# A two-layer hybrid trunk on one core: convolution and Fourier inputs as seven-product block multiplications, two conditioning groups on TensorE

## The chip, the cores and the metric

The kernel runs on one core of a Trainium2 chip. The metric is the device time of one execution in microseconds (us), median of three runs. The engines are named as the profile names them: PE is TensorE's matrix multiplication and PEld its weight load, DVE is VectorE, ACT ScalarE, POOL GpSimd, and SP SyncE, which here only issues DMAs.

## The reference

Two layers work on 640 tokens: 512 latent ones in four blocks of 128, and one block of 128 context tokens. The model width is 1024. Per layer:

```
h = LN0(x) * (1 + scale) + shift          # shift, scale, gate = silu(cond) @ w_mod + b_mod
q, k, v, z_a, cb, cc, cx, z_b, fx, z_c, g = split(h @ w_in)
                                          # widths 512,128,128,512, 4 x 512, 512,512, 3 x 1024
y_a = attention(q, k, v) * silu(z_a)      # 8 heads of 64, 2 KV heads, window +-128 and the context
y_b = cb * dwconv3(cc * cx) * silu(z_b)
y_c = Re(FFT2(fx by groups of 128)) * silu(z_c)
merged = sum over b of sigmoid(g_b) * (y_b @ w_branch_b)
x = LN(alpha * x + gate * (merged @ w_o)) * ln_g + ln_b
```

The outputs are the tokens after two layers and each layer's keys and values of the context block. All of it is float32.

## The kernel before

**Products.** Activations lie with channels on the partitions and tokens along the free axis. A float32 product is made of three products of a faster format: each operand is split into a high part (a copy on ACT) and a remainder (a subtraction on DVE, `split`, L147 for weights), and hi·hi, hi·lo and lo·hi are summed in PSUM. The input projection has 58 chunks of 128 columns, and eight k-steps of 128 rows. A plain chunk (`inproj`, `product`, L505 to L507) takes, per k-step, three matmuls of 256 and three of 384 tokens, 48 in all; its weights come in two 128x512 tiles, each of which is split.

**Pairs.** The 24 gate chunks go two at a time through a 2x2 block product with seven multiplications in place of eight (Strassen's scheme). The blocks are the two chunks, the two halves of the input channels, and the two halves of each token block (so 320 tokens). A seventh (L957) is 12 matmuls of 320 columns; three of seven read sums of input blocks, kept in tiles `T` (made by `sums` and `last_sum` on DVE and ACT), and the weights of three are sums of weight blocks (`Sum` on DVE; one sum, s1, by a DMA of POOL's queue that accumulates, L137). Results come in three banks, x, y and z, which ACT copies and DVE adds into two result rows.

**Stages of a layer.** First Q, K and V. Then attention in ten units (token block 0 to 4, KV head 0 or 1; a name ends in layer, block, head, and counter): `scores` on PE (L645), the mask with its maximum on DVE (L648), exponentials on ACT (L670, after a table load) with their sums, the normalisation by the reciprocal on POOL (L676, four instructions a unit); then `values`: four transposes of 128 columns on PE into pt (L694), a copy and subtraction into pT, and the products into po (L699 and L700). Between the units stand the 20 chunks of the A gating path and of the convolution (`fills`). Chunks 26 to 33 are the Fourier branch, each FX chunk followed by its transforms (`channels`, `positions`). Then the gates by pairs, in whose midst the branch projections (pb) are placed, then the output projection and the residual.

**Conditioning.** The shift, scale and gate vectors of both layers come from w_mod, in groups of 512 columns. Layer 0's first ones are done on PE at the start (modp L459, 256 columns, eight matmuls each; then modq). The others are accumulated on DVE: per k-step two instructions of 128x512 (L239, or L236 for the first), then a transpose, a reduction and one matmul. Groups (0,4), (0,5) and (1,0) do so beside layer 0's attention (`mod_steps`, rows `P<-sz`); the remaining ones beside the gates (`mod_piece`, rows `moda<-rawm`).

**Order.** The program is written as a list of jobs; `run` issues weight loads on SP's queue and weight splits as far ahead as six raw and five split tiles allow. The framework's scheduler then fixes each engine's order, so each engine runs its own list in order and waits on semaphores. SBUF is divided into large tiles with letters (A to F), each reused when its last reader is done; row tiles have five buffers. PSUM has two double banks (chunks) and four single ones (`aux`).

## Time and profile before

| | us |
|---|---|
| median of 3 runs (1242.32 to 1243.58) | 1242.64 |
| the profiled execution | 1243.65 |
| its span, first to last instruction | 1241.9 |
| PE busy | 1211.6 |
| DVE busy | 918.7 |
| ACT busy | 568.3 |
| POOL busy | 182.1 |

The span starts with the first instruction. Busy times of different engines lie beside each other. In a timeline, a row's second number is how long one instruction takes from its start to its end; where instructions follow each other without a gap, the distance between two starts is what one costs, and is shorter, since the next begins before the last has drained. A row ends in the idle time before it and what ended it, where there was any. PE's granted clock is given as a share of full speed: its mean over the span is 0.996.

### The profile page before, as it was taken

The numbers are of one execution on the slowest core, as the hardware profiler recorded it, in microseconds if no ns is written. First come the engines' busy times: TensorE is split into PE (matmuls) and PEld (weight loads), VectorE is DVE, ScalarE is ACT, GpSimd is POOL, SyncE is SP. The second block draws the span as 40 slices with busy tenths as digits, with TensorE's granted clock in tenths as the row PEclk, the third lists the DMA queues.
The fourth block names the chain that finished last, engine by engine and source line by source line (L and its number), as shares of the span: only waits on it lengthen the run. The fifth ranks groups of instructions, "written<-read, shape, count | busy, mean of one in ns | idle before, by whom it ended". The sixth has DMA issues, their size and how long they took to land.

```text
span 1241.9 us, 20937 instructions
## 1 busy us (share of the span) xinstructions
PE 1211.6 (98%) x8016; PEld 1166.8 (94%) x8016; DVE 918.7 (74%) x1683; ACT 568.3 (46%) x1100; POOL 182.1 (15%) x180
## 2 busy tenths in 40 slices
PE   5999999999999999999999999999999999999997
PEld 4899999999999999999889999999999999999986
DVE  5795697879799876677888665666869966666766
ACT  4345636456344344463245646545444344445300
POOL 2003424041000000000230324232000000000001
PEclk8999999999999999999999999999999999999999
DMA  9632131313255452453412211112223533433351
GB/s 353 235 113 69 52 119 60 102 60 120 62 160 153 128 151 71 102 174 135 158 72 82 73 56 60 51 55 93 92 57 125 160 111 92 131 88 106 105 187 51
DMA packets 64085, 137.38 MB, mean 111 GB/s; under 512 B 7600, under 2 KB 8176, under 8 KB 63728
## 3 DMA queue, kind: packets, MB, share of 16 engines
q1 hardware_dynamic: 59232, 125.35, 30.5%
q0 software_dynamic: 4176, 10.39, 4.1%
q8 instruction: 63, 1.03, 0.4%
q10 hardware_dynamic: 576, 0.30, 0.1%
q14 instruction: 38, 0.31, 0.1%
HBM read 130.48 MB, written 5.52 MB: 110 GB/s over the span
## 4 chain that ended last, share of the span: by engine, by line
PE 88%; DVE 6%; DMA 2%; issue 2%; ACT 1%; POOL 1%; DVEq 0%; SPq 0%; POOLq 0%
PE y L957 13%; PE p L505 12%; PE p L507 12%; PE p L506 12%; PE z L957 6%; PE pb L505 4%; PE pb L507 4%; PE pb L506 4%; PE x L957 3%; PE pt L694 2%; PE s L645 2%; PE p L422 2%; PE o L1118 2%; PE o L1117 2%; PE o L1119 2%
## 5 line engine op out<-in xcount | busy, mean ns | idle before, releaser
L505 PE MATMUL p<-act,hlw 128*128 128x256 f32 (+1 forms) x1024 | 321.0, 314 | 0.9 <-ACT qr L69 0.9
L507 PE MATMUL p<-act,hlw 128*128 128x256 f32 (+1 forms) x1024 | 318.9, 311 | 0.0
L506 PE MATMUL p<-act,hlw 128*128 128x256 f32 (+1 forms) x1024 | 317.4, 310 | 0.0
L505 PEld LDWEIGHTS p<-act,hlw 128*128 128x128 f32 x1024 | 193.3, 189 | 2.8 <-ACT qr L69 1.2
L506 PEld LDWEIGHTS p<-act,hlw 128*128 128x128 f32 x1024 | 192.8, 188 | 1.5
L507 PEld LDWEIGHTS p<-act,hlw 128*128 128x128 f32 x1024 | 192.8, 188 | 1.3
L676 POOL TENSOR_SCALAR P<-P,rc 128x384 f32<-128x384 f32 (+2 forms) x80 | 115.5, 1459 | 233.2 <-ACT hlw L69 101.4
L69 ACT ACTIVATE hlw<-raww 128x512 fp32r<-128x512 f32 x136 | 85.2, 629 | 109.0 <-PE p L507 97.0
L147 DVE TENSOR_TENSOR hlw<-raww,hlw 128x512 fp32r<-128x512 f32 x134 | 92.4, 693 | 25.0 <-ACT hlw L69 23.9
L1117 PE MATMUL o<-wo,act 128*128 128x512 f32 (+1 forms) x168 | 63.8, 381 | 0.0
L1118 PE MATMUL o<-wo,act 128*128 128x512 f32 (+1 forms) x168 | 63.5, 379 | 0.0
L1119 PE MATMUL o<-wo,act 128*128 128x512 f32 (+1 forms) x168 | 63.1, 379 | 0.0
L72 DVE TENSOR_TENSOR pT<-pt,pT 128x512 fp32r<-128x512 f32 x60 | 40.1, 685 | 20.9 <-ACT pT L69 20.8
L69 ACT ACTIVATE gs<-y 128x320 f32<-128x320 f32 x48 | 20.8, 433 | 67.3 <-PE y L957 66.3
L239 DVE SCALAR_TENSOR_TENSOR moda<-rawm,scond,moda 128x512 f32<-128x512 f32 x70 | 51.0, 742 | 0.0
L69 ACT ACTIVATE pT<-pt 128x512 fp32r<-128x512 f32 x60 | 34.9, 592 | 31.5 <-PE pt L694 25.0
L648 DVE CUSTOM_DVE_ANT_0 P<-s,mask 128x384 f32<-128x384 f32 (+1 forms) x64 | 38.5, 617 | 10.3 <-PE s L645 10.2
L670 ACT ACTIVATE P<-P,nm 128x384 f32<-128x384 f32 (+1 forms) x64 | 42.1, 658 | 1.2 <-DVE es L72 0.7
L75 DVE TENSOR_TENSOR gs<-pb,gs 128x640 f32<-128x640 f32 x16 | 13.2, 825 | 38.6 <-PE pb L507 38.6
L505 PE MATMUL pb<-ya,hlb 128*128 128x256 f32 (+1 forms) x128 | 40.1, 313 | 0.1
L505 PE MATMUL pb<-yc,hlb 128*128 128x256 f32 (+1 forms) x128 | 39.9, 311 | 0.0
L505 PE MATMUL pb<-yb,hlb 128*128 128x256 f32 (+1 forms) x128 | 39.8, 311 | 0.0
(722 smaller groups left out, 2888.5 us busy)
## 6 DMA issues: line engine op xcount, KB each, us to landing
raww<-in_w_in SPq DMA_DIRECT2D x136, 256.0 KB, 2.9
rawm<-in_w_mod SPq DMA_DIRECT2D x36, 512.0 KB, 4.3
rawg<-in_w_in SPq DMA_DIRECT2D x72, 256.0 KB, 3.4
rawb<-in_w_branch SPq DMA_DIRECT2D x48, 256.0 KB, 3.1
rawo<-in_w_o SPq DMA_DIRECT2D x32, 256.0 KB, 3.0
sz<-in_w_mod SPq DMA_DIRECT2D x24, 256.0 KB, 3.0
dft<-in_dft POOLq DMA_DIRECT2D x2, 1542.0 KB, 7.6
x<-in_x SPq DMA_DIRECT2D x5, 512.0 KB, 8.3
```

What stands on the lines that cost most here:

```text
L69: nc.scalar.activation(out, in_, AF.Copy)
L147: eng.tensor_tensor(out=self.hl[:, 1], in0=raw, in1=fr(self.hl[:, 0]), op=ALU.subtract)
L239: nc.vector.scalar_tensor_tensor(out=acc[:, c], in0=w, scalar=scond[:, k, c:c + 1], in1=acc[:, c], op0=ALU.mult, op1=ALU.add)
L505: nc.tensor.matmul(ps[:, a:b], lhsT=ld.w(0, k), rhs=mh, start=k == 0, stop=False)
L506: nc.tensor.matmul(ps[:, a:b], lhsT=ld.w(0, k), rhs=ml, start=False, stop=False)
L507: nc.tensor.matmul(ps[:, a:b], lhsT=ld.w(1, k), rhs=mh, start=False, stop=k == nk - 1)
L670: nc.scalar.activation(P[:, g, :W], srcs[g], AF.Exp, scale=0.125, bias=nm_[:, g:g + 1], accum_out=sm[:, g:g + 1])
L676: nc.gpsimd.tensor_scalar(out=P[:, g, :W], in0=P[:, g, :W], scalar1=rc[:, g:g + 1], scalar2=None, op0=ALU.mult)
L957: nc.tensor.matmul(out, lhsT=ld.w(z, k), rhs=moving(k, y), start=first and k == i == 0, stop=k == 3 and i == 2, skip_group_check=True)
L1117: nc.tensor.matmul(ps, lhsT=act[:, t, 0, k], rhs=w[:, 0], start=k == 0, stop=False)
L1118: nc.tensor.matmul(ps, lhsT=act[:, t, 0, k], rhs=w[:, 1], start=False, stop=False)
L1119: nc.tensor.matmul(ps, lhsT=act[:, t, 1, k], rhs=w[:, 0], start=False, stop=k == NK - 1)
```

## The change

Twelve more pairs per layer use the seven products: for the convolution, CC with CX and ZB with CB of each 128 channels (named c and d, with layer and number), and for the Fourier branch FX and ZC two by two (f). The code of a pair becomes the class `Pair`, with y and z in one double bank; the gates are `Gates(Pair)`. The four ZA chunks stay plain. The sums `T` are made at the start of attention rather than in the Fourier stage, and `fills` places six of a pair's sevenths after each unit. Conditioning groups (0,4) and (0,5) go to PE, 512 columns wide (`mod_group`); group (1,0) goes to the gates' pieces. y_a and y_b are kept unsplit and split beside the gates (`split_y`). The large tiles get other letters, and the loads of w_o other places. In the changed file lines are some six higher: L694 becomes L700, L699 becomes L705, and the line of a seventh, L957, becomes L827.

```diff
+    def mod_group(l, n, tag):
+        w = {}
+        def fetch():
+            w["raw"] = big.tile([128, 4096 if tag == "F" else 5120], F32, name=f"rawm{l}{n}", tag=tag)
+            for kp in range(4):
+                nc.sync.dma_start(out=w["raw"][:, kp * 1024:(kp + 1) * 1024], in_=I["w_mod"][l * 6 + n - 4, kp])
+        def rows():
+            pr = aux(f"modp{l}{n}")
+            for k in range(NK):
+                c = 32 * (k % 4)
+                nc.tensor.matmul(pr[c:c + 32], lhsT=scond32[:, k], rhs=w["raw"][:, k * 512:(k + 1) * 512],
+                                 start=k < 4, stop=k >= 4, tile_position=(0, c))
+            w["rows"] = row(f"modr{l}{n}")[:, 0:512]
+            copy(w["rows"], pr)
+        def columns():
+            ps = aux(f"modq{l}{n}")
+            for i in range(4):
+                nc.tensor.matmul(ps[:, 2 * i:2 * i + 2], lhsT=w["rows"][:, i * 128:(i + 1) * 128], rhs=pick,
+                                 start=True, stop=True)
+            add(modT[:, l, n * 4:(n + 1) * 4, :], ps[:, 0:8].rearrange("p (j s) -> p j s", s=2),
+                bmod[:, l, n * 4:(n + 1) * 4].unsqueeze(2).broadcast_to([128, 4, 2]))
+            mod_scale(l, n)
+        return fetch, rows, columns
...
-            S["ya"] = big.tile([128, 4, 2, TOK], F32R, name=f"ya{l}", tag="C")
-            P = big.tile([128, 5120], F32, name=f"P{l}", tag="E")
+        def begin_scores():
...
+        groups = [mod_group(0, 4, "T"), mod_group(0, 5, "F")] if l == 0 else []
...
-                    mul(ytv, ytv, S["sz"][:, :, tok])
-                    split(S["ya"][:, :, 0, tok], S["ya"][:, :, 1, tok], ytv)
+                    mul(S["sz"][:, :, tok], ytv, S["sz"][:, :, tok])
...
+        class Pair:
+            def __init__(self, nm, c0, c1, begin, done):
+                self.nm, self.begin, self.done, self.G, self.ps = nm, begin, done, [], {}
+                src = [[I["w_in"][l, c][:, h * 512:(h + 1) * 512] for h in range(2)] for c in (c0, c1)]
+                a11, a12 = (Raw(src[0][h], f"g{nm}1{h}") for h in range(2))
+                s1 = Raw(src[1][0], f"g{nm}s", src[1][1])
+                a22 = Raw(src[1][1], f"g{nm}22")
+                def hl(raw, frees, i):
+                    return Split(raw, f"g{nm}p{i}", frees)
+                def old(half, kh):
+                    return lambda k, z: act[:, :, z, 4 * kh + k, 64 * half:64 * half + 64]
+                def new(i):
+                    return lambda k, z: S["T"][i][:, z, k]
+                self.steps = [
+                    (Load([s1, a11, a12, a22], [hl(a11, [], 1)]), "y", old(0, 0), self.keep(0, 0)),
+                    (Load([], [hl(a12, [], 2)]), "x", old(0, 1), self.plus(0, 0)),
+                    (Load([], [hl(s1, [], 5), Sum(add, s1, s1, a11)]), "z", new(0), lambda out: None),
+                    (Load([], [hl(s1, [], 6), Sum(sub, a11, s1, a22), Sum(add, a12, a12, s1, [s1])]), "y", new(1),
+                     self.keep(0, 1)),
+                    (Load([], [hl(a11, [a11], 7)]), "y", new(2), self.third),
+                    (Load([], [hl(a22, [a22], 4)]), "y", lambda k, z: act[:, :, z, k, 64:128], self.last_y),
+                    (Load([], [hl(a12, [a12], 3)]), "z", old(1, 1), self.last_z)]
+            def place(self, bank):
+                if bank == "x":
+                    return aux(f"x{self.nm}")
+                if bank == "y":
+                    self.two = mmt(f"yz{self.nm}")
+                    return self.two[:, 0:512]
+                return self.two[:, 512:1024]
+            def emit(self, n=7):
+                for _ in range(n):
+                    ld, bank, moving, then = self.steps.pop(0)
+                    job(self.product(bank, moving, then), ld)
+            def product(self, bank, moving, then):
+                def body(ld):
+                    first = bank not in self.ps
+                    if first:
+                        self.ps[bank] = self.place(bank)
+                    out = self.ps[bank][:, :320]
+                    for k in range(4):
+                        for i, (z, y) in enumerate(((0, 0), (0, 1), (1, 0))):
+                            nc.tensor.matmul(out, lhsT=ld.w(z, k), rhs=moving(k, y), start=first and k == i == 0,
+                                             stop=k == 3 and i == 2, skip_group_check=True)
+                    then(out.rearrange("p (t i) -> p t i", i=64))
+                return body
+            def keep(self, i, half):
+                def then(out):
+                    if not self.G:
+                        self.G = self.begin()
+                    copy(quarter(self.G[i], half), out)
+                return then
+            def plus(self, i, half):
+                def then(out):
+                    add(quarter(self.G[i], half), out, quarter(self.G[i], half))
+                return then
+            def third(self, out):
+                self.keep(1, 1)(out)
+                self.plus(1, 1)(self.ps["z"][:, :320].rearrange("p (t i) -> p t i", i=64))
+            def last_y(self, out):
+                copy(quarter(self.G[1], 0), out)
+            def last_z(self, out):
+                self.plus(0, 1)(out)
+                self.done(*self.G)
...
+            return [Pair(f"c{l}{j}", C_CC + j, C_CX + j, two_rows("gc"), use_u),
+                    Pair(f"d{l}{j}", C_ZB + j, C_CB + j, two_rows("gd"), use_b)]
+        fill = [p for j in range(4) for p in conv(j) for _ in range(7)]
...
-        side = mod_steps(((0, 4), (0, 5), (1, 0)) if l == 0 else (), lambda: S["moda"], lambda: S["modr"])
...
+                    fill.pop(0).emit(1)
+        if l == 0:
+            job(groups[0][1])
         job(scores(0))
-        fills(2)
+        gating(0)
+        if l == 0:
+            job(groups[0][2])
+            job(groups[1][1])
+        gating(1)
+        if l == 0:
+            job(groups[1][2])
+        job(begin_sums)
+        job(sums(0))
         job(scores(1))
-        fills(1)
+        gating(2)
+        job(sums(1))
         for u in range(10):
             job(values(u))
-            beside(1)
+            if u == 0:
+                gating(3)
+                job(last_sum)
             if u + 2 < 10:
                 job(scores(u + 2))
-                fills(1)
-                beside(1)
-                fills(1)
-                beside(1)
-        beside(99)
+            fills(6 if u else 2)
...
+        def fourier_pair(c, i, use):
+            def begin():
+                return [S["G"][:, i + j] for j in range(2)]
+            g = i % 4
+            return Pair(f"f{l}{i}", c + g, c + g + 1, begin, lambda a, b: use((g, a), (g + 1, b)))
...
-        inproj(l, C_FX, use_fx(0))
-        job(begin_sums)
-        job(sums(0))
-        inproj(l, C_FX + 1, use_fx(1))
-        for g in range(4):
-            job(channels(g))
-            inproj(l, C_ZC + g, use_zc(g))
-            if g == 3:
-                job(last_sum)
-            job(positions(g))
-            if g == 0:
-                job(sums(1))
-            if g < 2:
-                inproj(l, C_FX + g + 2, use_fx(g + 2))
...
+        def split_y(y, tag):
+            def body():
+                w = big.tile([128, 4, 2, TOK], F32R, name=f"s{y}{l}", tag=tag)
+                src = S["sz" if y == "ya" else y]
+                S["s" + y] = w
+                for k in range(4):
+                    split(w[:, k, 0], w[:, k, 1], src[:, k])
...
+        p = fourier_pair(C_FX, 0, use_fx)
+        p.emit()
+        p = fourier_pair(C_ZC, 4, use_zc)
+        p.emit(4)
+        job(channels(0))
+        p.emit(2)
+        job(channels(1))
+        p.emit(1)
+        p = fourier_pair(C_FX, 2, use_fx)
+        p.emit(2)
+        job(positions(0))
+        p.emit(3)
+        job(positions(1))
+        p.emit(2)
+        p = fourier_pair(C_ZC, 6, use_zc)
+        p.emit(3)
+        job(channels(2))
+        p.emit(2)
+        job(channels(3))
+        p.emit(2)
+        job(positions(2))
+        job(positions(3))
+        pieces = [(1, n, kp) for n in (range(4) if l == 0 else (4, 5)) for kp in range(4)]
...
+                if (b, m) == (1, 0):
+                    job(split_y("yb", "C"))
                 piece()
-                if b == 2 and 1 <= m < 3:
-                    load_wo(0, "D", m - 1)
+                if b == 2:
+                    piece()
+                if (b, m) == (0, 1):
+                    job(split_y("ya", "A"))
+                if (b, m) in ((0, 2), (0, 3)):
+                    load_wo(1, "D", m - 2)
```

PE, in attention of layer 0. Before, around the first values of block 2: pt are transposes, po the products that read their copies pT, p0_16 a plain chunk of the convolution.

```order
L699 MATMUL po020_2010<-pT0201_2016,KV0_553 128x512
L694 MATMUL pt0202_2021<-ident_90,P0_560 128x128 x4
L694 MATMUL pt0203_2031<-ident_90,P0_560 128x128 x4
L507 MATMUL p0_16_2159<-act_109,hlw0_16_1_1996 128x384
L505 MATMUL p0_16_2159<-act_109,hlw0_16_1_1996 128x256
L506 MATMUL p0_16_2159<-act_109,hlw0_16_1_1996 128x256
L507 MATMUL p0_16_2159<-act_109,hlw0_16_1_1996 128x256
L505 MATMUL p0_16_2159<-act_109,hlw0_16_1_1996 128x384
L506 MATMUL p0_16_2159<-act_109,hlw0_16_1_1996 128x384
L507 MATMUL p0_16_2159<-act_109,hlw0_16_1_1996 128x384
L505 MATMUL p0_16_2159<-act_109,hlw0_16_1_1996 128x256
L700 MATMUL po020_2010<-pT0201_2016,KV0_553 128x512
```

Between the transposes of pt0202 and the first product that reads pT0202 stand 23 rows, ten of them shown here. After, at the first values of block 1 (yzd00 and yzc01 are sevenths of convolution pairs):

```order
L700 MATMUL pt0100_1601<-ident_90,P0_909 128x128 x4
L705 MATMUL po010_1600<-pT0100_1606,KV0_553 128x512
L827 MATMUL yzd00_1577<-tb0_1100,hlgd00p5_1526 128x320 x12
L827 MATMUL yzd00_1577<-tb0_1100,hlgd00p6_1543 128x320 x11
L700 MATMUL pt0101_1611<-ident_90,P0_909 128x128 x4
L700 MATMUL pt0102_1621<-ident_90,P0_909 128x128 x4
L827 MATMUL yzd00_1577<-tb0_1100,hlgd00p6_1543 128x320
L706 MATMUL po010_1600<-pT0100_1606,KV0_553 128x512
L700 MATMUL pt0103_1631<-ident_90,P0_909 128x128 x4
L705 MATMUL po010_1600<-pT0101_1616,KV0_553 128x512
L706 MATMUL po010_1600<-pT0101_1616,KV0_553 128x512
L651 MATMUL s0200_1644<-KV0_553,Q0_552 128x512 x2
```

The first value product stands directly behind the transposes whose copy it reads, and sevenths behind it.

DVE, in layer 0 between the maxima of the first unit (mx000, ahead of these rows) and those of the second (mx001). The sums of input blocks read `act`; ta, tb and tc are row tiles, tb0 and tf0 the tiles T. All of this stood in the Fourier stage before:

```order
L78 TENSOR_TENSOR ta01_1210<-act_109 128x5x2x64
L78 TENSOR_TENSOR tb01_1211<-act_109 128x5x2x64
L72 TENSOR_TENSOR tb00_1103<-tb00_1103,ta00_1102 128x640
L72 TENSOR_TENSOR tb01_1211<-tb01_1211,ta01_1210 128x640
L72 TENSOR_TENSOR ta00_1102<-tc00_1104,ta00_1102 128x640
L147 TENSOR_TENSOR hlw0_9_1_1086<-raww0_9_1_831,hlw0_9_1_1086 128x512
L72 TENSOR_TENSOR ta01_1210<-tc01_1212,ta01_1210 128x640
L72 TENSOR_TENSOR tb0_1100<-tb00_1103,tb0_1100 128x640
L743 SCALAR_TENSOR_TENSOR tc00_1104<-tc00_1104,tb00_1103 128x640
L72 TENSOR_TENSOR tb0_1100<-tb01_1211,tb0_1100 128x640
L72 TENSOR_TENSOR tf0_1101<-ta00_1102,tf0_1101 128x640
L743 SCALAR_TENSOR_TENSOR tc01_1212<-tc01_1212,tb01_1211 128x640
```

They stand in one piece, with one weight split (hlw0_9_1) among them.

POOL, in layer 0's attention. Before, the normalisations (TENSOR_SCALAR) follow each other with only the convolution's small memsets between:

```order
L676 TENSOR_SCALAR P0_560<-P0_560,rc020_1642 128x512 x4
L730 MEMSET u02_2208 128x2
L731 MEMSET u02_2208 128x1
L676 TENSOR_SCALAR P0_560<-P0_560,rc021_1871 128x512 x4
L676 TENSOR_SCALAR P0_560<-P0_560,rc030_2085 128x384 x4
L730 MEMSET u03_2635 128x2
L731 MEMSET u03_2635 128x1
L676 TENSOR_SCALAR P0_560<-P0_560,rc031_2314 128x384 x4
```

After, the accumulating DMAs of the pairs' weight sums (rawgc02s is that of pair c of layer 0, number 2) stand between them:

```order
L682 TENSOR_SCALAR P0_909<-P0_909,rc020_1672 128x512 x4
L137 DMA rawgc02s_1888<-in_w_in 128x512
L682 TENSOR_SCALAR P0_909<-P0_909,rc021_1863 128x512 x4
L862 MEMSET u01_2071 128x2
L863 MEMSET u01_2071 128x1
L137 DMA rawgd02s_2104<-in_w_in 128x512
L682 TENSOR_SCALAR P0_909<-P0_909,rc030_2052 128x384 x4
L137 DMA rawgc03s_2317<-in_w_in 128x512
L682 TENSOR_SCALAR P0_909<-P0_909,rc031_2248 128x384 x4
```

Each unit's normalisation now has one DMA ahead of it or behind it on POOL's queue.

## Rows read from the trace of the kernel before

**Rows 1.** The page, parts 1 and 2: busy shares; slices in tenths.

```profile
PE 1211.6 (98%) x8016; PEld 1166.8 (94%) x8016; DVE 918.7 (74%) x1683; ACT 568.3 (46%) x1100; POOL 182.1 (15%) x180
...
PE   5999999999999999999999999999999999999997
...
PEclk8999999999999999999999999999999999999999
```

**Rows 2.** PE's waits: line waited for, us in total, times, longest.

```profile
PE tr L342 <- DVE xn L328: 9.8, 2, 9.0
PE tr L342 <- ACT xn L326: 4.3, 2, 2.2
PE y L957 <- ACT gs L69: 2.6, 5, 0.5
```

**Rows 3.** Windows: length, busy us of PE, PEld, DVE, ACT, POOL; clock, DMA.

```profile
83.00:345.60 262.60, 262.47 (x1771) 255.99 (x1771) 206.25 (x419) 139.94 (x282) 65.69 (x59) 1.00 0.27 84
684.20:945.50 261.30, 261.17 (x1760) 254.83 (x1759) 174.30 (x360) 136.85 (x278) 62.12 (x57) 1.00 0.22 69
346.00:425.00 79.00, 76.46 (x516) 75.32 (x514) 76.35 (x126) 32.62 (x62) 3.46 (x4) 1.00 0.52 154
165.00:185.00 20.00, 20.00 (x137) 19.47 (x137) 19.90 (x43) 9.15 (x19) 4.89 (x2) 1.00 0.45 146
```

**Rows 4.** PE's timeline in a plain chunk: start, us.

```profile
67.15 0.34 PE L505 MATMUL p<-act,hlw 128*128 128x384 f32 x1
...
68.04 0.34 PE L505 MATMUL p<-act,hlw 128*128 128x384 f32 x1
```

**Rows 5.** PE's timeline in a gate pair.

```profile
375.38 1.92 PE L957 MATMUL x<-act,hlg012p 128*128 128x320 f32 x12
377.14 0.46 PE L957 MATMUL z<-tb,hlg012p 128*128 128x320 f32 x2
```

**Rows 6.** The chain that ended last, in two stretches: start, us, work.

```profile
22.30 1.01 PE modp L459 x8
...
153.41 0.87 PE pt L694 x8
```

**Rows 7.** DVE's timeline, in three stretches.

```profile
131.65 0.69 DVE L147 TENSOR_TENSOR hlw<-raww,hlw 128x512 fp32r<-128x512 f32 x1 [0.23 <-ACT hlw L69]
132.26 0.68 DVE L72 TENSOR_TENSOR pT<-pt,pT 128x512 fp32r<-128x512 f32 x1
...
346.22 0.82 DVE L72 TENSOR_TENSOR act<-td,act 128x640 fp32r<-128x640 f32 x1
346.96 0.74 DVE L239 SCALAR_TENSOR_TENSOR moda<-rawm,scond,moda 128x512 f32<-128x512 f32 x1
...
357.94 0.48 DVE L78 TENSOR_TENSOR gs<-z,gs 128x320 f32<-128x320 f32 x1
358.34 0.73 DVE L239 SCALAR_TENSOR_TENSOR moda<-rawm,scond,moda 128x512 f32<-128x512 f32 x1
359.00 0.68 DVE L72 TENSOR_TENSOR rawg<-rawg011s,rawg 128x512 f32<-128x512 f32 x1
```

**Rows 8.** Groups by form: DVE's conditioning in attention, ACT's copy of transposes.

```profile
L239 DVE SCALAR_TENSOR_TENSOR P<-sz,scond,P 128x512 f32<-128x512 f32 x42 | 30.4, 742 | 0.1
...
L69 ACT ACTIVATE pT<-pt 128x512 fp32r<-128x512 f32 x60 | 34.9, 592 | 31.5 <-PE pt L694 25.0 <-PE po L700 6.1
```

**Rows 9.** ACT's timeline, before the exponentials of unit (1,0).

```profile
126.61 1.28 ACT L670 ACT_TABLE_LOAD   x1
```

**Rows 10.** POOL's timeline, three stretches.

```profile
131.61 6.94 POOL L676 TENSOR_SCALAR P<-P,rc 128x512 f32<-128x512 f32 x4 [15.03 <-ACT hlw L69]
...
180.11 9.44 POOL L676 TENSOR_SCALAR P<-P,rc 128x512 f32<-128x512 f32 x4 [23.60 <-DVE rc L674]
...
358.92 0.86 POOL L137 DMA_DIRECT2D rawg012s<-in_w_in  x1 [39.69 <-DVE gs L78]
```

**Rows 11.** The page, part 6: gate weights' DMAs, count, KB, us to landing.

```profile
rawg<-in_w_in SPq DMA_DIRECT2D x72, 256.0 KB, 3.4
```

416 lines of the change are left out of this document (180 added, 236 removed).

## The prediction, made before the changed kernel ran

> **What bounds the kernel now.** I read first the page's busy shares and slices [rows 1]: TensorE (PE) is busy in 1211.6 of 1241.9 us, in nine tenths or more of every slice but the first and the last, with its clock granted in full after the first slice; VectorE (DVE) is at 74%, ScalarE (ACT) at 46%. Then PE's waits [rows 2]: the longest are the start's, for the normalised input, and after it no group of them is above 2.6 us. Then two windows that hold attention, convolution and Fourier of layers 0 and 1 [rows 3]: PE works 262.47 of 262.60 and 261.17 of 261.30 us. So the time is PE's instruction count times their prices, and any engine can be slower up to the point where PE waits for it. The third window is the gates with the conditioning sums: DVE at 76.35 of 79.00 us, and PE still works 76.46. That is the nearest thing the trace has to the stages that the change makes.
>
> **What comes off PE.** A plain chunk costs per k-step .89 us (from 67.15 to 68.04, six matmuls) [rows 4], so 8 × .885 = 7.08 us, and two chunks 14.16. Of a pair in seven products, twelve 320-column matmuls take 1.76 us (375.38 to 377.14) [rows 5]; seven are 12.32. Each pair saves 1.84 us; there are 8 convolution and 4 Fourier pairs in two layers, so 24 × 1.84 = 44.1 us.
>
> **What is put on PE.** Two conditioning groups: 8 matmuls of 512 columns and 4 tiny ones each. The trace has eight such of 256 columns in 1.01 us [rows 6], so 512 columns should take 2.0, two groups 4.0, and with the tiny ones 4.3 us. Bounds: 2.3 us if the width cost nothing (twice 1.01, and the tiny ones), 6 if it cost half as much again. Their 4 MB come on SP's queue behind the Q chunks; if they are late, the scores queued behind them on PE wait, which I count in the upper bound. No matmul is added elsewhere. PE's sum against the profiled execution: 1243.65 − 44.1 + 4.3 = 1203.9 us.
>
> **What DVE gets, and what hides it.** Its back-to-back pitches, from one start to the next [rows 7]: 512 wide .61 us (131.65 to 132.26; .60 in the sums below), 512 wide with two operators .66 (358.34 to 359.00), 640 wide .74 (346.22 to 346.96), 320 wide .40 (357.94 to 358.34). Two plain chunks need 4 weight splits (a subtraction each) on DVE, 2.4 us. A pair needs 7 splits, 3 block sums (an accumulating DMA makes a fourth) and 3 adds of 320 columns: 4.2 + 1.8 + 1.2 = 7.2 us. That is +4.8 per pair, +57.6 a layer. The conditioning in layer 0's attention leaves DVE: 42 instructions of one row [rows 8] and six first ones at .66, and three transposes with three reductions, some 1.2 us each as an allowance: 37 us. One of the three groups comes back in layer 0's later gates, 12 us of DVE; at the loss of the third window (2.5 in 76 us) that is under .5, and is left out. The splits of two branch inputs, 8 of 512 to 640 columns, 6 us, move to the gates too. So from first score to first gate product DVE would work 206.25 − 37 − 6 + 57.6 = 221 us in layer 0 and 174.3 − 6 + 57.6 = 226 in layer 1. PE's work there is 262.5 − 12 × 1.84 = 240.4, plus 4.3 in layer 0: DVE at 90% and 94%. In the third window of [rows 3] DVE at 97% cost PE 2.5 us in 79, which over 240 us would be 8 a layer. The average hides one place: the operand sums now stand between the first two units (the second of the order's places), 30 operations of 640 columns with those of the gating chunks, at .74: 22 us. Up to the second pair of the second channel block I count 60 us for DVE and 51 for PE, after a lead of some 13 us that DVE has from the first masks; 4 us of it are left. For all of attention in layer 0 DVE has 125 × .60 + 36 × .74 + 19 × .40 + masks and convolution taps 24 + small ones 6 = 140 us, PE 552 × .147 + 28.3 (four plain chunks) + scores and values 27 + 120 transposes 13 (eight in .87 [rows 6]) + 4.3 = 154. So DVE alone should make PE wait between 0 and 10 us a program; I take 4.
>
> **What the order makes PE wait for.** Two chains get less cover. *Values behind transposes.* A value product reads a copy that ACT makes of the transposes in .59 us [rows 8], with some .2 around it. Before, each of 60 stands at least 2.9 us of other PE work behind its transposes; now 11 of 60 stand under .8, eight of them directly behind (the first of the order's places). What is missing to .8 sums to 7.2 us. *Transposes behind scores.* After a unit's last score come mask, exponentials, and the normalisation on POOL. For unit (1,0) it took from ACT's table load at 126.61 [rows 9] to POOL's end at 138.55 (131.61 + 6.94), 11.9 us; POOL's four take 9.44 where DVE is saturated [rows 10] (in the fourth window of [rows 3] it works 19.90 of 20 us); with mask and maximum, .7, it is 12.6 to 15.1 us. Before, 14 to 30 us of PE work stood between; now (1,0) and (1,1) have 11.7 to 13.5 in both layers, the others 15.7 or more, and the last, narrow unit 8.2 against some 7.6 needed (an estimate: its exponentials and POOL's share by a quarter of the columns). Between 1 and 11 us in all; I take 6. POOL also has accumulating DMAs between normalisations now (the third place), which the trace of before has only in the gates; by bounds from the rows, nothing below; above, .9 us to issue one [rows 10], and 3.4 that the queue can stand until the first half has landed [rows 11]. With 9.44 + .9 + 3.4 it needs 13.7 us a unit against some 16 of PE's period; it is not late next as long as that holds. The row tiles, five buffers, are now shared with the pairs' results; I price that at 0 below and 5 above.
>
> **A rule of the Trainium skill weighed.** The trace first: while POOL normalises from 131.61 on [rows 10], DVE's weight split at 131.65, with two SBUF operands, keeps its pitch of .61 [rows 7], and where DVE is full POOL's four grow from 6.94 to 9.44. The page "SBUF — State Buffer" (section "Who interferes with whom") says that a DVE instruction with two SBUF inputs and a GpSimd instruction that reads SBUF exclude each other, and whichever starts first blocks the other outright. By it the loss may fall on DVE as well; the trace so far shows it on POOL alone. By the row the stalls are 17 us, as above; by the rule, were the loss DVE's, they would grow to the 42 us of the last rival but one.
>
> **Sum.** 1203.9 + 7 (values) + 6 (transposes) + 4 (DVE) = 1221 us for a profiled execution. That of before lay 1.0 us above the median of its three runs, so 1220.
>
> **The rivals.**
> *All gaps hidden* (chance .18): the scheduler's order is kept busy by queued matmuls, as the third window of [rows 3] suggests; stalls 0 to 7: 1203 to 1210 us. For it: PE's waits before are nearly nil. Against: 11 products that stand right behind their source can't avoid the copy.
> *DVE or the chains are late all along* (.21): DVE at 94% works in order, and one late exponential delays splits queued behind it. Stalls of 25 to 36 us, at the upper bounds of the terms (10 DVE + 11 transposes + 9 values + 5 rows): 1228 to 1239 us.
> *Slower than before* (.08): POOL and DVE exclude each other to DVE's cost. POOL is busy 65.69 us in the first window [rows 3]; some six tenths of DVE's work has two SBUF operands, so up to 35 to 39 us a layer would be added to DVE's 140 in attention, 175 against PE's 154: 21 a layer, 42 in all, 1203.9 + 42 = 1246 us, slower by 2 to 3. It is what the page named above would allow. The point at which it decides is 40 us of stalls, 20 a layer. Against it: DVE's pitch beside POOL, unchanged [rows 7].
> *Not what it says*: if seven products didn't cost less than two chunks there would be no change; [rows 4, 5] exclude that, so .02 for a gain eaten to within .2%.
>
> **How the numbers follow.** The forecast case, stalls of 9 to 24 us, has .51: 1212 to 1227. The range that leaves out no more than two tenths runs from 1205 to 1240: some .08 lies below (the better half of the first rival), .1 above (slower, or hardly faster). A change of under .2%, 2.5 us, could not be told from none here. Faster by more than that, below 1240.1: .18 + .51 + .19 = .88; within: .04; slower: .08.
>
> **What would show it.** Right: about 242 us instead of 262 from a layer's first scores to its first gate product; DVE near 90% there; PE's new waits named as values for ACT's copies and transposes for POOL, 7 and 6 us; the granted clock still 1.00. Wrong: PE waiting for DVE's weight splits in attention by more than 10 us; POOL's four longer than 10 us, or DVE's 512-wide pitch above .65 beside them; the 512-column conditioning matmuls waiting for their DMA; or seven products in more than 12.5 us.

## The result, and the profile after

The changed kernel takes **1286.45 us** (median of four runs, 1282.6 to 1288.12) against 1242.7 us for the kernel before on the same chip: ratio **1.0347 [1.0323, 1.037]**, slower by 3.5%, where 1220 was forecast. Its profiled execution, the fastest of the four, took 1282.6 us, with a span of 1280.8 and a mean granted clock of 0.987 (before 0.996).

The page after, parts 1 and 2, as [rows 1] showed them before:

```profile
PE 1198.8 (94%) x7772; PEld 1134.2 (89%) x7772; DVE 1011.1 (79%) x1855; ACT 622.0 (49%) x1236; POOL 200.1 (16%) x204
...
PE   6999888989999999999989979998999999999997
...
PEclk9999999999999999999989999999999999999998
```

PE works less than before, but by 12.8 us, not by the 39.8 of the sum (44.1 − 4.3), and it is idle for 82.0 us (1280.8 − 1198.8) where it was 30.3. Eights and a seven stand in slices that were nines. The sum without stalls was 1203.9; the excess over it, 78.7 us, is 51.7 of idle time and 27.0 of work that took longer than its price.

PE's waits after, which answer to [rows 2] (line waited for, us in total, times, longest):

```profile
PE po L705 <- ACT pT L69: 15.5, 10, 3.8
PE yzc L827 <- ACT gc L69: 15.3, 13, 2.2
PE tr L318 <- DVE xn L304: 9.2, 1, 9.2
PE tr L318 <- ACT xn L302: 6.6, 3, 4.4
PE yzd L827 <- ACT gd L69: 3.8, 5, 1.0
...
PE po L706 <- DVE pT L72: 2.4, 5, 1.0
```

Values (po) wait for copies of the transposes, sevenths (yzc, yzd) for copies of a bank of their own pair (gc and gd are its result rows, which ACT copies from y). No row names POOL, and the longest wait for a weight split is 1.8.

Four stretches show where this lies: from a layer's first scores to its first gate product, from there to the next layer's first scores, the same again, and the last from layer 1's first gate product to the end. The answer's columns are those of [rows 3]. First the kernel before, cut at the exact starts (the windows of [rows 3] ended some us later):

```profile
83.00:339.33 256.33, 256.33 (x1731) 250.12 (x1731) 199.98 (x408) 136.18 (x273) 65.69 (x59) 1.00 0.26 81
339.33:684.57 345.24, 341.08 (x2216) 328.84 (x2216) 272.92 (x450) 153.82 (x291) 30.45 (x31) 1.00 0.41 127
684.57:940.48 255.91, 255.91 (x1726) 249.84 (x1725) 168.94 (x351) 133.71 (x269) 62.12 (x57) 1.00 0.21 67
940.48:1241.90 301.42, 290.52 (x1855) 279.61 (x1854) 216.02 (x346) 110.14 (x206) 15.41 (x15) 0.99 0.38 117
```

And after:

```profile
82.94:353.34 270.40, 247.01 (x1617) 231.59 (x1613) 223.52 (x452) 157.05 (x332) 70.66 (x70) 0.99 0.28 76
353.34:711.55 358.21, 346.33 (x2218) 332.90 (x2218) 289.60 (x478) 156.56 (x296) 29.59 (x29) 0.99 0.41 126
711.55:978.47 266.92, 245.45 (x1581) 232.21 (x1581) 223.73 (x453) 156.84 (x331) 74.96 (x71) 0.98 0.29 78
978.47:1280.80 302.33, 290.44 (x1855) 279.68 (x1854) 215.35 (x349) 113.41 (x211) 15.50 (x15) 0.99 0.37 114
```

By the prices, the two attention stretches should hold 256.33 + 255.91 − 44.1 + 4.3 = 472.4 us of PE work. They take 537.3: 492.5 of work and 44.9 idle. That is 65 of the 78.7. The second stretch is 13.0 longer (idle 11.9 instead of 4.2, and 5.3 more work; the granted clock was 0.50 over 660 to 666 us); it holds the gates, the output projection and the residual, on which the change adds nothing to PE. The fourth is 0.9 longer.

Why a seventh waits is seen at the first pair. PE's timeline after, around 120 us (start, us):

```profile
121.10 1.18 PE L827 MATMUL yzc<-act,hlgc00p 128*128 128x320 f32 x7
...
125.69 3.79 PE L827 MATMUL yzc<-tb,hlgc00p 128*128 128x320 f32 x24 [1.79 <-ACT gc L69]
```

ACT's timeline after, in the same stretch:

```profile
121.42 1.28 ACT L676 ACT_TABLE_LOAD   x1
122.71 0.62 ACT L676 ACTIVATE P<-P,nm 128x384 f32<-128x384 f32 x1
...
125.13 0.19 ACT L676 ACTIVATION_READ_ACCUMULATOR P<-P,nm 128x1 f32 x1
125.22 0.42 ACT L69 ACTIVATE gc<-yzc 128x320 f32<-128x320 f32 x1
```

The product into y ends near 122.3. Its copy gc is queued on ACT behind a table load and four exponentials, so it starts at 125.22 and the next product into the double bank at 125.69. The first twelve of those 24 matmuls go into z, not y.

Later PE's speed falls behind some of the waits. Windows after, around 260 us (the seventh number is the granted clock):

```profile
258.00:260.00 2.00, 0.83 (x2) 0.20 (x2) 0.65 (x2) 1.99 (x3) 0.85 (x2) 1.00 0.40 120
260.00:264.00 4.00, 3.79 (x15) 3.80 (x16) 3.20 (x5) 1.04 (x3) 0.76 (x4) 0.57 0.78 178
```

PE's timeline over that stretch:

```profile
257.83 0.50 PE L705 MATMUL po<-pT,KV 128*128 128x512 f32 x1 [1.23 <-ACT pT L69]
258.56 0.49 PE L706 MATMUL po<-pT,KV 128*128 128x512 f32 x1 [0.23 <-DVE pT L72]
260.20 5.32 PE L827 MATMUL yzc<-tb,hlgc03p 128*128 128x320 f32 x24 [1.15 <-ACT gc L69]
```

After three waits in 4 us the granted clock is 0.57 over the next four, that is mostly the lower level, 1.2 GHz, and 24 matmuls that took 3.79 at 125.69 take 5.32. Not every wait does this: over the 4 us from 125.70 on, behind the wait of 1.79, the clock stayed 1.00. Before, both attention windows of [rows 3] stood at 1.00. A mean of 0.987 over 1280.8 us against 0.996 over 1241.9 is 16.7 − 5.0 = 11.7 us of full-speed time, an estimate from the rounded means, and a bound from above, since the slow stretches also hold idle time.

### The profile page after: what moved, and what is told of

The parts are those of the page before. It is cut to its first block, busy times and chain, and to the rows that moved or that the text cites. A ratio compares the mean times of both kernels' runs of the same rounds, so it can differ in the third digit from the quotient of the medians.

```text
span 1280.8 us, 20819 instructions
## 1 busy us (share of the span) xinstructions
PE 1198.8 (94%) x7772; PEld 1134.2 (89%) x7772; DVE 1011.1 (79%) x1855; ACT 622.0 (49%) x1236; POOL 200.1 (16%) x204
## 3 DMA queue, kind: packets, MB, share of 16 engines
q1 hardware_dynamic: 57504, 125.35, 29.4%
## 5 line engine op out<-in xcount | busy, mean ns | idle before, releaser
L509 PE MATMUL p<-act,hlw 128*128 128x256 f32 (+1 forms) x256 | 80.5, 314 | 0.0
L511 PE MATMUL p<-act,hlw 128*128 128x256 f32 (+1 forms) x256 | 79.7, 311 | 0.0
L510 PE MATMUL p<-act,hlw 128*128 128x256 f32 (+1 forms) x256 | 79.2, 309 | 0.0
L239 DVE SCALAR_TENSOR_TENSOR moda<-rawm,scond,moda 128x512 f32<-128x512 f32 x84 | 61.2, 744 | 0.4 <-DMA rawm<-in_w_mod 0.4
L509 PEld LDWEIGHTS p<-act,hlw 128*128 128x128 f32 x256 | 48.4, 189 | 1.1 <-issue 0.8
L511 PEld LDWEIGHTS p<-act,hlw 128*128 128x128 f32 x256 | 48.2, 188 | 0.0
L510 PEld LDWEIGHTS p<-act,hlw 128*128 128x128 f32 x256 | 48.2, 188 | 0.0
L69 ACT ACTIVATE hlw<-raww 128x512 fp32r<-128x512 f32 x40 | 25.0, 631 | 32.1 <-PE p L511 19.3
L705 PE MATMUL po<-pT,KV 128*128 128x512 f32 x60 | 25.7, 428 | 15.6 <-ACT pT L69 15.5
L147 DVE TENSOR_TENSOR hlb<-rawb,hlb 128x512 fp32r<-128x512 f32 x48 | 33.0, 687 | 9.3 <-ACT hlb L69 9.1
L509 PE MATMUL pb<-sya,hlb 128*128 128x256 f32 (+1 forms) x128 | 40.1, 313 | 0.1
L69 ACT ACTIVATE hlb<-rawb 128x512 fp32r<-128x512 f32 x48 | 30.1, 627 | 20.3 <-PE z L827 8.0
```

Of the source, the lines that this page charges most:

```text
L69: nc.scalar.activation(out, in_, AF.Copy)
L239: nc.vector.scalar_tensor_tensor(out=acc[:, c], in0=w, scalar=scond[:, k, c:c + 1], in1=acc[:, c], op0=ALU.mult, op1=ALU.add)
L509: nc.tensor.matmul(ps[:, a:b], lhsT=ld.w(0, k), rhs=mh, start=k == 0, stop=False)
L510: nc.tensor.matmul(ps[:, a:b], lhsT=ld.w(0, k), rhs=ml, start=False, stop=False)
L511: nc.tensor.matmul(ps[:, a:b], lhsT=ld.w(1, k), rhs=mh, start=False, stop=k == nk - 1)
```

## The experiments

Times are medians; changes are against the changed kernel's 1286.45 unless said otherwise, and ratios against the kernel before on the same chip. The changed kernel's own runs spread over 5.5 us.

**e1_out_order.** The changed kernel also issues the output projection one block further ahead, which the prediction passed over. Undone:

```diff
-        job(oproj(2, 0))
         job(residual(0, 0))
...
-                if t + 2 < NT:
-                    job(oproj(t + 2, 0))
+                job(oproj(t + 1, 0))
```

> The changed kernel (1286.4 us) with the output projections in the order of the kernel before: the third token block's first half is not pulled ahead. Between layer 0's first gate product and layer 1's first scores the changed kernel lost some 13 us, of which PE's idle time at 630 to 672 us is 7 and a fallen clock behind it 3. Theory that the order of the output stage does this: 8 to 12 us faster, 1275 us. Rival, that the tiles' new letters make the loads of w_o late: no change, within 2 us.

1280.67 us, ratio 1.0312 [1.0296, 1.0327]: 5.7 us of the loss, less than the 8 to 12 expected.

**e2_conv_plain.** The convolution's chunks plain again; the Fourier pairs stay. (Its convolution reads input blocks that the operand sums have by then overwritten, so its values differ.)

```diff
-        fill = [p for j in range(4) for p in conv(j) for _ in range(7)]
+            filler(C_CC + j, use_cc)
+            filler(C_CX + j, use_cx)
+            filler(C_CB + j, use_cb)
+            filler(C_ZB + j, use_zb)
...
-                    fill.pop(0).emit(1)
+                    inproj(l, *fill.pop(0))
...
-            fills(6 if u else 2)
+            fills(2)
```

> The changed kernel with the 16 chunks of the convolution plain again in attention, two after each unit; the Fourier pairs, the operand sums at the start, the conditioning on TensorE and the tiles stay. PE's own work grows by 16 x 1.84 = 29 us. Theory that the convolution's pairs make PE wait in attention (ACT's copies late, too little other PE work between): the two attention stages give back 50 to 60 us, and the time falls to 1255 to 1265 us. Rival, that the operand sums at the start and the full DVE are the cause: they stay, so the stalls stay, and the time is 1290 us or more.

1261.02 us, ratio 1.0155 [1.014, 1.017]: 25.4 us faster with 16 × 1.84 = 29.4 us more work for PE. The convolution's pairs cost some 55 us of waiting and slower work; PE's wait for pT falls to 1.7 us.

**e3_exp_narrow and e4_exp_by_head.** Is it the exponentials' row on ACT? One makes them 64 columns wide, the other releases each head's exponential by its own maximum.

```diff
-                    nc.scalar.activation(P[:, g, :W], srcs[g], AF.Exp, scale=0.125, bias=nm_[:, g:g + 1],
+                    nc.scalar.activation(P[:, g, :64], srcs[g][:, :64], AF.Exp, scale=0.125, bias=nm_[:, g:g + 1],
```

```diff
                 for g in range(4):
-                    nc.scalar.activation(P[:, g, :W], srcs[g], AF.Exp, scale=0.125, bias=nm_[:, g:g + 1],
-                                         accum_out=sm[:, g:g + 1])
+                    c = slice(g, g + 1)
+                    nc.vector.scalar_tensor_tensor(out=mx[:, c], in0=mx[:, c], scalar=0.125, in1=ns[:, c], op0=ALU.mult,
+                                                   op1=ALU.max)
+                    nc.vector.tensor_scalar(out=nm_[:, c], in0=mx[:, c], scalar1=-1.0, scalar2=None, op0=ALU.mult)
+                    nc.scalar.activation(P[:, g, :W], srcs[g], AF.Exp, scale=0.125, bias=nm_[:, c], accum_out=sm[:, c])
```

> The changed kernel with each exponential over 64 columns in place of 128 to 512 (the rest of the scores is left as it is and clamped at the normalisation, so the attention is not computed); all other instructions stay, with one small DVE addition per unit. It shortens ACT's four exponentials from 2.8 us or so to about 1, with the table load still ahead. Theory that PE waits because ACT's copies of PSUM stand behind a table load and four exponentials: 20 to 35 us faster, 1252 to 1266 us, and PE's waits for ACT in attention fall by more than half. Rival, that DVE is the limit or that the products stand too close even for a free ACT: less than 8 us faster.

> The changed kernel with the exponential of each head issued as soon as that head's maximum is known, in place of four in a row after all four maxima: the same work, and six small DVE instructions more a unit (some 12 us of DVE in all). In the order the copies of PSUM now stand between the exponentials. Theory of ACT's row of exponentials: PE's longest waits for ACT fall from 4 us to 1 or 2, 10 to 25 us faster, 1262 to 1276 us. Rival, DVE as the limit: 5 to 12 us slower, 1291 to 1298 us.

1282.33 (1.0328 [1.0309, 1.0346]), 4 us faster, and 1292.2 (1.0404 [1.0387, 1.0422]), 5.8 slower. The exponentials' length is not the main thing; the second came out as its rival, DVE as the limit, had it. The first is weakened by clamping at the normalisation on POOL, busy 227.1 us instead of 200.1, and by one more small instruction on DVE a unit.

**e5_no_block_sums and e6_rc_on_pool.** Is it DVE's fill? One leaves out the pairs' block sums of weights, the other moves the sum and the reciprocal of the softmax to POOL.

```diff
         def emit(self):
-            self.op(*(r.tile for r in self.raws))
+            if self.raws[0].nm[1] not in "cdf":
+                self.op(*(r.tile for r in self.raws))
```

```diff
-                add(sm, sm, es)
+                nc.gpsimd.tensor_tensor(out=sm, in0=sm, in1=es, op=ALU.add)
...
-                nc.vector.reciprocal(out=rc, in_=sm)
+                nc.gpsimd.tensor_tensor(out=rc, in0=sm, in1=none4, op=ALU.pow)
```

> The changed kernel without the three block sums of weights on DVE in the convolution and Fourier pairs (their products use unsummed weights, so those values are not the reference's): 1.8 us less DVE work a pair, 14 us less a layer in attention and 7 in the Fourier stage; ACT, PE and POOL have the same work. Theory that DVE's fill makes the copies and splits late and PE waits for it, directly or through ACT: 15 to 35 us faster, 1250 to 1270 us. Rival, that the products stand too close behind ACT's copies whatever DVE does: less than 8 us faster.

> The changed kernel with the sum and the reciprocal of the softmax on POOL (two instructions of 128x4) in place of DVE, where they stood waiting for ACT's exponentials: 15.8 us of standstill in layer 0's attention, eight waits. Theory of DVE's fill: DVE is then never held by an exponential, the work queued behind it starts earlier, 10 to 25 us faster, 1262 to 1276 us. Rival, closeness behind ACT's copies: within 4 us of 1286; if POOL's two small instructions cost 1.4 us each, up to 10 slower.

1284.05 (1.034 [1.031, 1.037]) and 1287.01 (1.035 [1.0308, 1.0393]): 2.4 faster and 0.6 slower, inside the spread of the changed kernel's own runs. What these two take off DVE doesn't carry the loss as the kernel stands.

**e7_hl4.** One split-weight tile fewer (`N_HL = 4`), to see whether weights come late.

```diff
-N_HL = 5
+N_HL = 4
...
-                    behind = ("hi", "lo") if 4 < split < 8 else ()
+                    behind = ("hi", "lo") if 4 < split < 8 and "lo" in last else ()
```

> The changed kernel with four tiles for split weights in place of five. A seventh uses one of them for 1.76 us, where a plain chunk used two for 7.1, so five tiles reach half as far ahead in time as before. Theory that this short reach makes PE wait: four tiles lose 15 us or more, 1300 us or more. Rivals (DVE's fill; closeness behind ACT's copies): less than 8 us slower.

1293.62 (1.0413 [1.0395, 1.0431]), 7.2 slower: inside what the rivals allowed (less than 8), half of what too short a reach was to cost (15). The opposite edit, more tiles, wasn't tried.

**e8_fills5.** Five sevenths after each unit instead of six: attention's own steps stand closer together, and what is left runs by itself behind them.

```diff
-            fills(6 if u else 2)
+            fills(5 if u else 0)
```

> The changed kernel with five sevenths after each unit in place of six, none after the first, and the rest behind attention. In the order the value products that stand under .8 us behind their transposes fall from 11 to 7, and what all 60 are short of 3 us falls from 50 to 40 us; the sevenths of a pair stand as before. Theory of closeness behind ACT's copies: 5 to 12 us faster, 1274 to 1281 us. Rival, DVE's fill: within 4 us.

1300.53 (1.0464 [1.0441, 1.0488]), 14 us slower, which neither theory had. The trace puts it behind attention and not in it. Up to a layer's last value product PE is idle 17.2 and 18.5 us in the two layers, in the changed kernel 18.6 and 16.7; from there to the first Fourier product 7.7 and 7.7, where it was 2.7 and 2.7. The sevenths that now stand alone wait for the copies of their own pair (yzc for gc 18.1 us, before this edit 15.3).

**e9_keep_on_dve and e10_pt_on_dve.** The copies that PE waits for, moved from ACT to DVE: those out of y for the convolution's pairs, or that of the transposes.

```diff
+                if self.nm[0] in "cd":
+                    nc.vector.tensor_copy(out=out, in_=in_)
+                else:
+                    copy(out, in_)
```

```diff
-                    split(pT[:, 0:512], pT[:, 512:1024], pt)
+                    nc.vector.tensor_copy(out=pT[:, 0:512], in_=pt)
+                    sub(pT[:, 512:1024], pt, fr(pT[:, 0:512]))
```

> The changed kernel with the copies of a convolution pair's y bank (four a pair) on DVE in place of ACT. PE and ACT now wait for each other in attention: PE for ACT's copies of y (11.4 us in layer 0), ACT for the products that it copies (12.7 us), in two queues that each run in order. Theory of this lock-step between PE and ACT: with the copies on DVE, which had room (leaving out 1.8 us of DVE a pair changed nothing), PE's waits for y fall by half and the time by 8 to 20 us, 1266 to 1278 us. Rival, that any engine's copy comes too late where the next seventh stands so close: within 4 us of 1286, with the waits now named for DVE.

> The changed kernel with the copy of the transposes (pT, the high part) on DVE in place of ACT: DVE gets 9 us more a layer by .6 us each, ACT as much less. Lock-step between PE and ACT: PE's waits for pT, 5.6 us in layer 0 and 9.9 in layer 1, fall by half: 5 to 12 us faster. Rival, closeness whatever the engine: within 4 us, waits named for DVE.

1299.09 (1.0464 [1.0434, 1.0494]) and 1295.88 (1.0426 [1.0408, 1.0445]): 12.7 and 9.5 slower, where no theory had more than 4. PE's waits in the first:

```profile
PE yzd L827 <- DVE gd L841: 12.5, 8, 3.1
...
PE yzc L827 <- DVE gc L78: 8.4, 7, 2.2
...
PE yzc L827 <- DVE gc L841: 5.7, 6, 2.0
```

The wait goes with the copy to the other engine. So it isn't ACT in particular: whichever engine empties the bank does so in order, behind its other work.

**e11_double_first.** Each convolution pair's first product into y made twice (the second restarts the bank): 16 × 1.76 = 28 us of work that adds nothing but cover, that is, something for PE to do while a copy is made.

```diff
+                    for n in range(2 if first and bank == "y" and self.nm[0] in "cd" else 1):
```

> The changed kernel with the first seventh of each convolution pair computed twice into the same bank (the second overwrites the first): 12 more matmuls of 320 columns, 1.76 us, in each of 16 pairs, 28 us of PE work that nothing waits for in addition. Theory of too little PE work between dependent steps (cover): the added work fills PE's idle time and the time grows by less than 12 us, under 1298 us. Rival, that PE's own rate or work sets the time there: 25 us or more, 1311 us.

1300.92 (1.0474 [1.0458, 1.0491]): 14.5 us slower for 28 of work. Half of it replaced waiting, which fits neither side's number; in the two attention stretches PE is idle 34.7 us instead of 44.9.

**e12_z_apart.** z in a single bank of its own; y alone in the double one.

```diff
                 if bank == "y":
-                    self.two = mmt(f"yz{self.nm}")
-                    return self.two[:, 0:512]
-                return self.two[:, 512:1024]
+                    return mmt(f"y{self.nm}")[:, 0:512]
+                return aux(f"z{self.nm}")
```

> The changed kernel with a pair's z in a PSUM bank of its own from the four single ones, not in the second half of y's double bank. In the order the third product of a pair then waits for DVE's split in place of ACT's copy of y. Theory that the shared tile makes z wait for y's copies: 5 to 12 us faster. Rivals: within 4 us, or slower by up to 10 since the single banks also serve scores and transposes.

1264.77 us, ratio 1.0186 [1.0167, 1.0205]: 21.7 us faster, twice what was expected. PE's waits:

```profile
PE po L705 <- ACT pT L69: 8.6, 6, 3.8
...
PE yc L826 <- ACT gc L69: 6.2, 8, 1.8
PE s L651 <- DVE mx L654: 5.7, 5, 1.7
...
PE zc L826 <- DVE gc L78: 1.7, 2, 0.9
```

The 15.3 us of yzc for gc become 6.2 of y alone, and the values wait 8.6 instead of 15.5 though nothing of theirs was edited: a pair's stalls, or the order that came of them, had delayed them too. The scores' wait for the maximum is new, 5.7 us: z now takes one of the four single banks that scores use. In the two attention stretches PE is idle 32.2 us instead of 44.9. The rule in the Trainium skill, page "PSUM — Partial Sum Buffer", section "PSUM bank collisions raise a hardware error", is to guard PSUM by bank and quadrant; y and z, each 512 columns of the double bank, would by it need no guard against each other. The trace agrees for z: with two tiles its first product starts without a wait, as the second of these rows shows.

```profile
125.81 2.03 PE L826 MATMUL yc<-tb,hlgc00p 128*128 128x320 f32 x12 [1.79 <-ACT gc L69]
146.62 1.91 PE L826 MATMUL zc<-tb,hlgc00p 128*128 128x320 f32 x12
```

But at this pair the wait of 1.79 stays, since y's own next product now stands there, and z's comes 21 us later. The edit changed the order as well: behind a layer's last value product 6.5 us are left until the first Fourier product, where the changed kernel has 20.7 and 19.2. So the 21.7 us are those of the two tiles and the order that follows from them; the runs don't part the two. That the framework tracks the double tile as one is argued from this, not read in a row.

**e13_z_out.** Both edits, e12's and e1's (their diffs).

> The changed kernel with z in a bank of its own and with the output projections in the order of before, the two edits of e12 and e1 together. If they act at different places and add up: 1264.8 - 5.7 = 1259 us, 1257 to 1261. If the second only moves a wait that the first has moved already: 1264.

1256.04 us, ratio 1.0109 [1.0094, 1.0124]: 30.4 us faster, 3 more than the two added up, a difference within the runs' spread; the output order is worth 8.7 here.

**e14_z_out_nosums.** e13 with e5's edit.

> e13 without the three block sums of weights in the convolution and Fourier pairs (1.8 us of DVE a pair, so those values are not the reference's). In e12 PE's idle time in layer 0's attention had DVE busy for 15.3 of 16.1 us and ACT for 12.5, where before the edit ACT was busy in all of it. Theory that with z apart DVE's fill is what is left: 8 to 20 us faster than e13. Rival, closeness of the order whichever engine: within 4 us of e13.

1248.18 us, ratio 1.0048 [1.0033, 1.0063]: 7.9 faster than e13, where the same edit gave 2.4 with z shared. DVE's fill shows once z no longer waits for y's copy. The edit takes 1.8 of the 4.8 us that a pair adds on DVE, in the Fourier pairs too; from a layer's first scores to its first Fourier product the two layers are 7.6 us shorter than in e13.

**e15_z_out_convplain.** e13 with e2's edit.

> e13 with the convolution's 16 chunks plain in attention, as in e2 (they read an input block that the operand sums have overwritten, so the values are not the reference's). PE's work grows by 29 us against e13. e2 took 1261.0 us with z in y's bank and the changed output order; less 6 for the order and 0 to 4 for the Fourier pairs' z: 1251 to 1255 us. Then the convolution's pairs still lose some 6 us even with z apart. Rival, that z apart makes them worth their saving: e15 is slower than e13, 1262 us or more.

1240.75 us, ratio 0.9988 [0.9978, 0.9997]: 15.3 us faster than e13, with 29.4 more of work, and 10 below what was expected. The two attention stretches of e13, in windows:

```profile
82.62:346.46 263.84, 247.69 (x1617) 231.84 (x1613) 222.79 (x450) 156.76 (x332) 77.60 (x70) 0.99 0.28 78
...
694.34:953.60 259.26, 242.85 (x1582) 230.18 (x1581) 223.17 (x451) 156.44 (x331) 77.09 (x71) 0.99 0.29 80
```

And of e15:

```profile
82.68:337.78 255.10, 253.53 (x1713) 244.68 (x1709) 182.75 (x378) 137.67 (x286) 65.82 (x63) 1.00 0.23 72
...
685.39:937.57 252.18, 250.03 (x1677) 242.31 (x1677) 183.45 (x379) 136.93 (x285) 64.71 (x63) 1.00 0.23 74
```

In e15 PE works 503.6 us, idle 3.7; by the prices (8 Fourier pairs, and 5.7 for the conditioning, below) it should work 512.2 − 14.7 + 5.7 = 503.2. In e13 it should work 29.4 less, 473.8; it works 490.5 and is idle 32.6. So the convolution's pairs, with z apart, still cost 29 us of waiting and 17 of slower work, 46 in all, and save 29.

**e16_before_ahead.** The kernel before, with only the output order of the changed one (the inverse of e1's diff).

> The kernel before, with only the output projections in the changed order (the third token block's first half ahead of the first residual, the others one block earlier). Theory that this order alone leaves PE without work at the layer's end: 4 to 8 us slower, 1246 to 1250 us. Rival, that it costs only beside the rest of the change: within 2 us of 1242.

1253.08 us against 1242.63, ratio 1.0084 [1.0067, 1.0101]: 10.4 us slower, more than the 4 to 8 expected. Its second stretch:

```profile
338.30:691.75 353.45, 343.31 (x2216) 330.34 (x2216) 273.14 (x450) 153.45 (x291) 30.17 (x31) 1.00 0.38 124
```

Its waits:

```profile
PE tr L342 <- ACT xn L326: 6.2, 3, 4.4
PE o L1117 <- ACT hv L355: 2.3, 2, 1.2
```

8.2 us longer than before's 345.24, of it 6.0 idle. The wait of 4.4 us, for the normalised input of the next layer, and the one for hv are those of the changed kernel's own list.

**e17_fourier_only.** What the runs point to, computing the reference: e15, with the operand sums moved behind the convolution's last readers of their blocks.

```diff
-        job(begin_sums)
-        job(sums(0))
         job(scores(1))
...
-        job(sums(1))
...
-                job(last_sum)
+            if u == 4:
+                job(begin_sums)
+            if u in (4, 6):
+                job(sums(u // 2 - 2))
...
-            fills(2)
+            fills(2 if u < 6 else 1)
         fills(99)
+        job(last_sum)
```

> A version that computes the reference: plain convolution chunks (two after each of the first six units, one after each later one), the operand sums at the fifth and seventh unit and the last behind the last chunk, Fourier pairs with z in a bank of its own, the output projections in the order of before, the conditioning on TensorE. PE's work is that of e15, 29 us more than the changed kernel's and 9 us less than before. If the late sums are hidden by the chunks: 1239 to 1243 us, at or a little below before. If the first Fourier pair waits for the last sums: 1244 to 1256 us.

1238.39 us against 1242.08, ratio **0.9974 [0.9963, 0.9986]**: 3.7 us faster than the kernel before. Its first three stretches:

```profile
82.66:336.82 254.16, 253.06 (x1712) 244.68 (x1709) 182.91 (x380) 140.04 (x288) 66.51 (x63) 1.00 0.23 73
336.82:684.95 348.13, 342.41 (x2218) 329.15 (x2218) 286.72 (x478) 156.78 (x296) 30.09 (x31) 1.00 0.41 130
684.95:934.49 249.54, 249.19 (x1678) 242.38 (x1677) 183.85 (x381) 139.23 (x287) 67.14 (x61) 1.00 0.24 75
```

PE is idle 1.5 us in the two attention stretches together. Against the kernel before they are 2.2 and 6.4 us shorter; the prices say 4 × 1.84 = 7.4 a layer, less 5.7 for conditioning in the first, so 1.7 and 7.4. The stretch between them is 2.9 us longer than before's 345.24, with 13.8 us more on DVE, where the conditioning group and the splits now stand.

## Why the prediction was wrong

**What held.** The prices on PE: e15's and e17's work comes out within 1 us of them. The work on DVE between first scores and first gate product, nearly: 223.5 and 223.7 us where 221 and 226 were forecast, though from windows that ended 6 and 5 us late; from the exact ones (199.98 and 168.94) the same sum gives 214.6 and 220.5. DVE's share was 83 and 84% only because the stretch grew. PE's wait for weight splits in attention is 0.4 us in the longest such row; more than 10 was a sign of being wrong.

**What was mis-sized.** The conditioning. PE's timeline after (one of two groups):

```profile
81.09 1.92 PE L464 MATMUL modp<-rawm,scond 128*32 128x512 f32 x16
91.53 0.95 PE L472 MATMUL modq<-pick,modr 128*128 128x2 f32 x8
```

That is 2.9 a group, 5.7 in all for 4.3: the wide matmuls cost what was forecast, the tiny ones 1.9 in place of 0.3. The work moved to the gates was priced at under 0.5; with the output order of before, that stretch is still 2.9 us longer (e17). The values: 15.5 + 2.4 us for pT where the working had 7. It counted the copy's 0.59 + 0.2 us, not what stands on ACT ahead of it. Two of the working's sums are off by little: its 37 us for the conditioning on DVE make 39 by its own terms, its upper stalls 35 and not 36.

**What didn't come.** Transposes waiting for POOL, 6 us. POOL's timeline after:

```profile
137.03 6.79 POOL L682 TENSOR_SCALAR P<-P,rc 128x512 f32<-128x512 f32 x4 [3.15 <-ACT hlgd00p L69]
...
155.39 6.18 POOL L682 TENSOR_SCALAR P<-P,rc 128x512 f32<-128x512 f32 x4 [4.12 <-ACT pT L69]
```

Its four of 512 columns take 6.2 to 7.5 us, not 9.44, and the accumulating DMAs 0.86 and 0.92 to issue. The working put the 9.44 down to a saturated DVE. That was a misreading: the window with DVE at 19.90 of 20 us ends 5 us into those four. Windows before, over the four of 9.44 and over the four of 6.94:

```profile
180.11:189.55 9.44, 9.44 (x60) 8.98 (x59) 8.31 (x16) 1.84 (x3) 9.44 (x6) 1.00 0.42 139
131.61:138.55 6.94, 6.94 (x49) 6.65 (x48) 6.90 (x13) 2.84 (x6) 6.94 (x4) 1.00 0.36 116
```

DVE is busy for 88% of the slow ones and 99% of the fast ones, so its share isn't what makes them slow.

**What came and was priced at nothing.** DVE's timeline beside POOL:

```profile
129.89 0.68 DVE L147 TENSOR_TENSOR hlgc00p<-rawgc,hlgc00p 128x512 fp32r<-128x512 f32 x1
130.50 0.68 DVE L654 CUSTOM_DVE_ANT_0 P<-s,mask 128x512 f32<-128x512 f32 x1
...
139.22 1.03 DVE L72 TENSOR_TENSOR rawgd<-rawgd00s,rawgd 128x512 f32<-128x512 f32 x1
140.17 0.68 DVE L78 TENSOR_TENSOR rawgd<-rawgd,rawgd00s 128x512 f32<-128x512 f32 x1
140.77 0.68 DVE L72 TENSOR_TENSOR pT<-pt,pT 128x512 fp32r<-128x512 f32 x1
```

Its pitch is .61 from 129.89, as in [rows 7], but .95 from 139.22, where POOL normalises too. By a count of DVE's rows in the two attention stretches, 62 instructions of 128x512 with both operands in SBUF run beside POOL's normalisation, and 23 of them take more than .65 to the next start, up to 1.15; of 152 beside no normalisation none does, nor any of 28 beside it that read PSUM. So this sign of being wrong did come. But it adds up to 6.5 us of DVE's work in two layers, where the rival that ended slower had 35 to 39 a layer: that rival had the right sign, and a mechanism that is there at under a tenth of its size. Of the rule in the Trainium skill, page "SBUF — State Buffer", section "Who interferes with whom", this trace shows delays on DVE in that case, but not that each such instruction waits out POOL's, which take 1.56 each where nothing slows them: 39 of the 62 keep their pitch.

**The step that failed** is "What the order makes PE wait for". It priced two chains, each by its own length, and three things stood outside it:

- *A pair's own steps.* Sevenths of 1.76 us follow each other into banks that ACT and DVE empty in order. With y and z in one double bank, a product into z also waited for y's copy. Parting them, with the order that follows, gives back 21.7 us of the loss (e12); the section on the change names the double bank, and the prediction gave it no price.
- *The cover that left.* Plain chunks of 7 us stood between attention's steps, read no fresh result and let their banks wait. The pairs take them away, and put sevenths there that wait as well. With z apart this still costs 46 us (e13 against e15), more than the 29 saved. The pairs' block sums on DVE are some 8 of it (e14). Moving copies between engines makes it worse (e9, e10), and extra work on PE is half hidden (e11). That the pairs cost this is shown; that it is the cover, more than a pair's own steps, is argued, for sevenths that stand behind attention by themselves wait as well (e8).
- *The output order.* It stood in the changed code outside the parts that I costed: 5.7 us (e1), 8.7 with z apart (e13 against e12), 10.4 by itself (e16).

A fourth follows from these: slower work behind waits. PE's busy time is 27.0 us over its sum: 1.4 is conditioning and at most 11.7 the clock, by the estimate above. The remaining 14 or more I haven't put down to single rows.

The working argued that DVE at 97% in the gates cost PE only 2.5 us, and took the same for attention. But there PE's next steps are pairs of the same kind, while attention puts a chain through ACT, DVE and POOL between them. PE's waits of nearly nothing in [rows 2] said that the cover was enough, not how much of it was needed.

**Open.** How the remaining 38 us of the convolution's pairs (46 − 7.9) divide between attention's chain and the pair's own evictions: in e13 PE waits 9.3 us for pT on ACT, 8.1 for y's copies and 4.9 for mask and maximum, and each of them can delay the next. What the rest of DVE's added work costs (3.0 us a pair beside the block sums), and the row tiles that the pairs share (0 to 5 us in the working), was not tested apart.
